# Weighted sum of two expert outputs: whole-tile VectorE instructions and results packed into the input tile

## The chip, the cores and the metric

The kernel runs on one core of one Trainium2 chip. The time is in device microseconds (us) of one execution; the median over several executions is what is compared. A profile of one execution, taken by the hardware, gives the span of the core, the busy time of each engine and every DMA's transfers. The span in a profile is about 2 us shorter than the time, since it starts with the first instruction.

Of the engines, VectorE (DVE) and ScalarE (ACT) compute here. SyncE (SP) only issues DMAs, and ScalarE issues DMAs too. Each of the two has a DMA queue of its own, and both queues are worked off by the same 16 DMA engines.

## The reference

Each of 16 x 1024 = 16384 tokens has the outputs of two experts, 512 values each, and two weights. The result is their weighted sum, in float32 throughout.

```python
batch, seq, hidden, n_experts, k = 16, 1024, 512, 8, 2
expert_outputs   # (batch, seq, k, hidden), float32
combine_weights  # (batch, seq, k), float32

def reference(expert_outputs, combine_weights):
    weights = combine_weights[..., np.newaxis]
    return np.sum(expert_outputs * weights, axis=2).astype(np.float32)
```

67.1 MB are read and 33.6 MB are written, with three arithmetic operations per result.

## The kernel before

128 partitions hold 128 tokens each, in 16 tiles of J = 8 tokens per partition. One tile is one load of 4 MB (32 KB per partition, contiguous in memory) and one store of 2 MB. Tiles are counted from 0; tile 15 is the last (`g == last`). Loads are issued by SyncE, stores by ScalarE, but for the four quarter stores of the last tile, which SyncE issues.

```python
    wpool = ctx.enter_context(tc.tile_pool(name="w", bufs=1))
    ipool = ctx.enter_context(tc.tile_pool(name="in", bufs=4))
    opool = ctx.enter_context(tc.tile_pool(name="out", bufs=4))

    wt = wpool.tile([P, per * k], dt)          # all weights, loaded once by two DMAs
    # ... cut: the two loads of wt, issued by ScalarE

    for g in range(per // J):
        et = ipool.tile([P, J, k * h], dt)     # 128 x 8 x 1024
        ot = opool.tile([P, J, h], dt)         # 128 x 8 x 512
        nc.sync.dma_start(out=et, in_=eo(g * J, J))
        c0 = 0
        for c in (2, 2, 2, 2) if g == last else (J,):
            for i in range(c0, c0 + c):
                t = g * J + i
                w0, w1 = wt[:, 2 * t : 2 * t + 1], wt[:, 2 * t + 1 : 2 * t + 2]
                if t == 0 or g == last:
                    nc.scalar.activation(out=ot[:, i, :], in_=et[:, i, 0:h], func=copy, scale=w0)
                else:
                    nc.vector.tensor_scalar_mul(out=ot[:, i, :], in0=et[:, i, 0:h], scalar1=w0)
                nc.vector.scalar_tensor_tensor(
                    out=ot[:, i, :], in0=et[:, i, h : 2 * h], scalar=w1, in1=ot[:, i, :],
                    op0=mult, op1=add,
                )
            (nc.sync if g == last else nc.scalar).dma_start(
                out=o(g * J + c0, c), in_=ot[:, c0 : c0 + c, :]
            )
            c0 += c
```

The kernel is written for a layer that orders the instructions of each engine by a scheduler of its own and sets the semaphores; a tile from a pool with `bufs=4` shares four buffers with the other tiles of that pool, and waits until the buffer it takes is no longer in use.

Of the kernel before, what the change touches and what calls it, by code (L numbers as in the profile page):

```python
# [1 line left out]

# [4 lines left out]


@with_exitstack
def kernel(  # L10
    ctx: ExitStack,
    tc: tile.TileContext,
    expert_outputs: bass.AP,
    combine_weights: bass.AP,
    out: bass.AP,
):

    nc = tc.nc  # L20
    b, s, k, h = expert_outputs.shape
    assert k == 2
    n = b * s
    P = nc.NUM_PARTITIONS
    per = n // P
    assert per * P == n
    J = 8
    main = per - J
    eo = expert_outputs.rearrange("b s k h -> (b s) (k h)")
    cw = combine_weights.rearrange("b s k -> (b s) k")  # L30
    o = out.rearrange("b s h -> (b s) h")

    def rows(x):

        a = x[0 : P * main, :].rearrange("(p t) f -> p t f", p=P)
        b = x[P * main : n, :].rearrange("(p t) f -> p t f", p=P)
        return lambda t, c: a[:, t : t + c, :] if t < main else b[:, t - main : t - main + c, :]

    eo, cw, o = rows(eo), rows(cw), rows(o)

    dt = mybir.dt.float32
    mult = mybir.AluOpType.mult
    add = mybir.AluOpType.add
    copy = mybir.ActivationFunctionType.Copy

    last = per // J - 1

    wpool = ctx.enter_context(tc.tile_pool(name="w", bufs=1))
    ipool = ctx.enter_context(tc.tile_pool(name="in", bufs=4))
    opool = ctx.enter_context(tc.tile_pool(name="out", bufs=4))  # L50

    wt = wpool.tile([P, per * k], dt)
    for t, c in ((0, main), (main, J)):
        nc.scalar.dma_start(
            out=wt[:, k * t : k * (t + c)].rearrange("p (t k) -> p t k", k=k), in_=cw(t, c)
        )

    for g in range(per // J):
        et = ipool.tile([P, J, k * h], dt)
        ot = opool.tile([P, J, h], dt)  # L60
        nc.sync.dma_start(out=et, in_=eo(g * J, J))  # L61
        c0 = 0
        for c in (2, 2, 2, 2) if g == last else (J,):
            for i in range(c0, c0 + c):
                t = g * J + i
                w0, w1 = wt[:, 2 * t : 2 * t + 1], wt[:, 2 * t + 1 : 2 * t + 2]


                if t == 0 or g == last:
                    nc.scalar.activation(out=ot[:, i, :], in_=et[:, i, 0:h], func=copy, scale=w0)  # L70
                else:
                    nc.vector.tensor_scalar_mul(out=ot[:, i, :], in0=et[:, i, 0:h], scalar1=w0)  # L72
                nc.vector.scalar_tensor_tensor(  # L73
                    out=ot[:, i, :],
                    in0=et[:, i, h : 2 * h],
                    scalar=w1,
                    in1=ot[:, i, :],
                    op0=mult,
                    op1=add,
                )  # L80

            (nc.sync if g == last else nc.scalar).dma_start(  # L82
                out=o(g * J + c0, c), in_=ot[:, c0 : c0 + c, :]
            )
            c0 += c


# [1 line left out]
_INS = ['expert_outputs', 'combine_weights']  # L89
_OUTS = [((16, 1024, 512), 'float32')]  # L90


# [23 lines left out]
```

## Time and profile before

| | |
|---|---|
| time, median of 3 runs | 241.44 us (241.16 to 241.47) |
| span of the profiled execution | 239.5 us |
| VectorE busy | 133.3 us, 56% of the span, 247 instructions |
| ScalarE busy | 7.0 us, 3%, 10 instructions |
| moved by DMA | 100.81 MB, mean 421 GB/s over the span |
| loads of a tile, issue to landing (min / median / max) | 12.6 / 49.5 / 50.5 us |
| stores, issue to landing (min / median / max) | 4.7 / 24.0 / 25.0 us |
| chain of work that ended last | DMA loads 56%, VectorE 26% of the span |
| first load landed, VectorE's first instruction | 13.37 us, 13.50 us |
| last store issued | 233.8 us |

Busy time counts an engine's instructions only, not what it waits for. A DMA's time to landing counts from its issue, so it holds the wait behind earlier DMAs of its queue as well as its own transfer. In the slices of the profile each digit is the busy share in tenths. Line numbers (L72, L73) are those of the kernel before: L72 is `tensor_scalar_mul`, L73 is `scalar_tensor_tensor`, L70 the activation, L61 the load, L82 the stores.

### The profile page before, as it was taken

The numbers are of one execution on the slowest core, as the hardware profiler recorded it, in microseconds if no ns is written. First come the engines' busy times: TensorE is split into PE (matmuls) and PEld (weight loads), VectorE is DVE, ScalarE is ACT, GpSimd is POOL, SyncE is SP. The second block draws the span as 40 slices with busy tenths as digits, with TensorE's granted clock in tenths as the row PEclk, the third lists the DMA queues.
The fourth block names the chain that finished last, engine by engine and source line by source line (L and its number), as shares of the span: only waits on it lengthen the run. The fifth ranks groups of instructions, "written<-read, shape, count | busy, mean of one in ns | idle before, by whom it ended". The sixth has DMA issues, their size and how long they took to land.

```text
span 239.5 us, 382 instructions
## 1 busy us (share of the span) xinstructions
DVE 133.3 (56%) x247; ACT 7.0 (3%) x10; POOL 0.2 (0%) x4
## 2 busy tenths in 40 slices
DVE  0077928529185490945819277291852918549080
ACT  0030000000000000000000000000000000000080
POOL 0000000000000000000000000000000000000000
DMA  7999899999999999999999999999999999999995
GB/s 268 451 441 439 350 438 476 401 432 424 411 441 435 479 394 438 435 441 400 435 438 441 435 460 413 438 402 432 437 435 479 397 438 427 449 397 435 438 409 213
DMA packets 5330, 100.81 MB, mean 421 GB/s; under 512 B 720, under 2 KB 848, under 8 KB 1360
## 3 DMA queue, kind: packets, MB, share of 16 engines
q1 hardware_dynamic: 2880, 69.21, 67.6%
q10 hardware_dynamic: 2448, 31.59, 30.9%
q14 instruction: 2, 0.02, 0.0%
HBM read 67.24 MB, written 33.55 MB: 421 GB/s over the span
## 4 chain that ended last, share of the span: by engine, by line
DMA 56%; DVE 26%; another core or an unknown queue 13%; issue 1%; SPq 0%; ACT 0%; DVEq 0%; ACTq 0%
DMA et<-in_expert_outputs_dram 56%; DVE ot L73 17%; DVE ot L72 10%; SPq L61 0%; ACT ot L70 0%; DVEq L111 0%; ACTq L82 0%; DVEq L72 0%; ACTq L70 0%
## 5 line engine op out<-in xcount | busy, mean ns | idle before, releaser
L72 DVE TENSOR_SCALAR ot<-et,wt 128x512 f32<-128x512 f32 x119 | 52.3, 481 | 93.7 <-DMA et<-in_expert_outputs_dram 80.2
L73 DVE SCALAR_TENSOR_TENSOR ot<-et,wt,ot 128x512 f32<-128x512 f32 x128 | 89.8, 745 | 6.7 <-ACT ot L70 6.7
L70 ACT ACTIVATE ot<-et,wt 128x512 f32<-128x512 f32 x9 | 5.7, 709 | 212.2 <-DMA et<-in_expert_outputs_dram 212.2
L70 ACT ACT_TABLE_LOAD x1 | 1.3, 1283 | 13.4 <-DMA et<-in_expert_outputs_dram 13.4
L100 POOL MEMSET const-bfloat16-1.0<- 128x1 bf16 x1 | 0.1, 102 | 0.0
L100 POOL MEMSET const-uint8-127<- 128x1 uint8 x1 | 0.1, 102 | 0.0
L100 POOL MEMSET const-float32-0.0<- 128x1 f32 x1 | 0.1, 99 | 0.2 <-issue 0.2
L100 POOL MEMSET const-float32-1.0<- 128x1 f32 x1 | 0.1, 99 | 0.0
## 6 DMA issues: line engine op xcount, KB each, us to landing
et<-in_expert_outputs_dram SPq DMA_DIRECT2D x16, 4096.0 KB, 49.5
out_dram<-ot ACTq DMA_DIRECT2D x15, 2048.0 KB, 24.1
out_dram<-ot SPq DMA_DIRECT2D x4, 512.0 KB, 4.9
wt<-in_combine_weights_dram ACTq DMA_DIRECT2D x1, 120.0 KB, 12.8
wt<-in_combine_weights_dram ACTq DMA_DIRECT2D x1, 8.0 KB, 22.1
```

The source lines that it names most:

```text
L70: nc.scalar.activation(out=ot[:, i, :], in_=et[:, i, 0:h], func=copy, scale=w0)
L72: nc.vector.tensor_scalar_mul(out=ot[:, i, :], in0=et[:, i, 0:h], scalar1=w0)
L73: nc.vector.scalar_tensor_tensor(out=ot[:, i, :], in0=et[:, i, h : 2 * h], scalar=w1, in1=ot[:, i, :], op0=mult, op1=add,)
L100: nc = _bacc.Bacc("TRN2", target_bir_lowering=False, num_devices=1)
```

## The change

Three things change together. First, each tile but the last is computed by two VectorE instructions in place of sixteen: one product of the whole tile with the weights, each weight repeated 512 times along its row by an access pattern of step 0, and one sum of the two halves of all eight tokens. Second, the result goes back into the input tile: the sum writes the eight results packed into the first half of `et`, so that each partition's 16 KB leave as one contiguous row. There is no output pool any more, and the freed memory makes six input buffers in place of four. Third, a tiny activation at the start brings ScalarE's table load forward. The last tile is still computed token by token by ScalarE and VectorE, with its results packed in place, and leaves in four quarters.

The aim is fewer and longer instructions on VectorE and loads that can run further ahead.

```diff
-    ipool = ctx.enter_context(tc.tile_pool(name="in", bufs=4))
-    opool = ctx.enter_context(tc.tile_pool(name="out", bufs=4))
+    ipool = ctx.enter_context(tc.tile_pool(name="in", bufs=6))
...
+    warm = wpool.tile([P, 1], dt)
+    nc.scalar.activation(out=warm, in_=nc.const_aps.tensor(1.0, (P, 1), dt), func=copy)
+
     for g in range(per // J):
         et = ipool.tile([P, J, k * h], dt)
-        ot = opool.tile([P, J, h], dt)
+        ot = et.rearrange("p j f -> p (j f)")[:, 0 : J * h].rearrange("p (j f) -> p j f", f=h)
         nc.sync.dma_start(out=et, in_=eo(g * J, J))
-        c0 = 0
-        for c in (2, 2, 2, 2) if g == last else (J,):
-            for i in range(c0, c0 + c):
...
-                if t == 0 or g == last:
-                    nc.scalar.activation(out=ot[:, i, :], in_=et[:, i, 0:h], func=copy, scale=w0)
-                else:
-                    nc.vector.tensor_scalar_mul(out=ot[:, i, :], in0=et[:, i, 0:h], scalar1=w0)
...
+        if g < last:
+            wb = wt[:, g * J * k : (g + 1) * J * k].unsqueeze(2).to_broadcast([P, J * k, h])
+            ek = et.rearrange("p j (k h) -> p (j k) h", k=k)
+            nc.vector.tensor_tensor(out=ek, in0=ek, in1=wb, op=mult)
+            nc.vector.tensor_tensor(out=ot, in0=et[:, :, 0:h], in1=et[:, :, h : 2 * h], op=add)
+            nc.scalar.dma_start(out=o(g * J, J), in_=ot)
+            continue
...
+        for c0 in range(0, J, 2):
+            for i in range(c0, c0 + 2):
+                t = g * J + i
+                nc.scalar.activation(
+                    out=et[:, i, 0:h], in_=et[:, i, 0:h], func=copy, scale=wt[:, 2 * t : 2 * t + 1]
+                )
                 nc.vector.scalar_tensor_tensor(
                     out=ot[:, i, :],
                     in0=et[:, i, h : 2 * h],
-                    scalar=w1,
-                    in1=ot[:, i, :],
+                    scalar=wt[:, 2 * t + 1 : 2 * t + 2],
+                    in1=et[:, i, 0:h],
                     op0=mult,
                     op1=add,
                 )
...
+            nc.sync.dma_start(out=o(g * J + c0, 2), in_=ot[:, c0 : c0 + 2, :])
```

## The prediction

> **What bounds the kernel now.** I read the page's table of slices first. Columns: one digit or number per 6 us slice.
>
> ```profile
> DVE  0077928529185490945819277291852918549080
> DMA  7999899999999999999999999999999999999995
> GB/s 268 451 441 439 350 438 476 401 432 424 411 441 435 479 394 438 435 441 400 435 438 441 435 460 413 438 402 432 437 435 479 397 438 427 449 397 435 438 409 213
> ```
>
> VectorE rests in every third slice; the DMA engines never do from the second slice to the last but one. Then the busy time by stages (stretch, its length, busy time and instruction count of each engine, clock, mean share of the 16 DMA engines, rate):
>
> ```profile
> 36.00:222.00 186.00, 111.24 (x208) 0.00 (x0) 0.00 (x0) 1.00 1.01 434
> 222.00:228.00 6.00, 0.00 (x0) 0.42 (x1) 0.00 (x0) 1.00 0.92 393
> 228.00:237.00 9.00, 5.39 (x8) 4.58 (x8) 0.00 (x0) 1.00 0.92 381
> 237.00:239.50 2.50, 0.00 (x0) 0.00 (x0) 0.00 (x0) 1.00 0.03 11
> ```
>
> In the long middle the rate is 434 GB/s at full DMA share, with VectorE busy 60%. Even while the last tile is computed (228 to 237) the engines are 0.92 full. Transfers run from about 1.6 to 237 us: 100.81 MB / 235.4 us = 428 GB/s on average. The bytes over that rate are the bound, and only time in which no transfer is queued can be added or removed. Next the queues and the DMA issues (median us to landing last):
>
> ```profile
> q1 hardware_dynamic: 2880, 69.21, 67.6%
> q10 hardware_dynamic: 2448, 31.59, 30.9%
> ...
> et<-in_expert_outputs_dram SPq DMA_DIRECT2D x16, 4096.0 KB, 49.5
> out_dram<-ot ACTq DMA_DIRECT2D x15, 2048.0 KB, 24.1
> ```
>
> A load is issued 49.5 us before it lands, over three tiles ahead, so the load queue is never empty. The packet counts give the arbitration: 16 loads x 128 rows + 4 last stores x 128 rows + 20 DMAs x 16 completions = 2880, and 15 x 128 + 256 + 17 x 16 = 2448. So a row is a packet: 32 KB in the load queue, 16 KB in the store queue. Last, the groups (count, then busy us and mean ns):
>
> ```profile
> L72 DVE TENSOR_SCALAR ot<-et,wt 128x512 f32<-128x512 f32 x119 | 52.3, 481 | 93.7 <-DMA et<-in_expert_outputs_dram 80.2
> L73 DVE SCALAR_TENSOR_TENSOR ot<-et,wt,ot 128x512 f32<-128x512 f32 x128 | 89.8, 745 | 6.7 <-ACT ot L70 6.7
> ```
>
> Neighbours overlap: in the timeline tile 2 runs from 36.86 to 45.41, so 8.55 us of VectorE per tile, against a load landing every (227.5 - 36.86) / 13 = 14.66 us.
>
> **What the Trainium skill says.** (1) "DMA: Bandwidth & Descriptors", section "Queues, rings and completion order": each DMA engine takes turns between its queues packet by packet. With rows of 32 and 16 KB that gives loads two thirds of the rate while stores are queued: 4.194 MB / (434 x 2/3) = 14.5 us per load, and the trace has 14.66. (2) The same page, "Where 436 GB/s comes from", puts the ceiling at 435 GB/s; the trace has 434, so no faster transfer is left to gain. (3) "VectorE: DVE Perf Modes", section "The TRN2 errata": an fp32 tensor_tensor takes (N + 151) / 0.96 ns. No tensor_tensor is in this trace, but the scalar_tensor_tensor, which also reads two fp32 streams, fits with N = 512: 691 ns by the formula, 745 in the trace. (4) "SBUF — State Buffer", section "SBUF: two separate sides": engines and DMA do not slow each other there. The trace agrees loosely: the rate of a slice does not follow VectorE's digit.
>
> **The change part by part.** *VectorE.* Per tile, 16 instructions go and 2 come: a product over 8192 elements and a sum over 4096. 512 elements at 0.96 per ns are 533 ns of the 745, so the fixed part is 212 ns; the product is then an estimated 8533 + 212 = 8.75 us and the sum 4267 + 212 = 4.48 us, together 13.2 us in place of 8.55. For 15 tiles that is +70 us of VectorE work, but 13.2 is still under 14.66, so it hides beside transfers. Fewer instructions save nothing that counts.
>
> *Buffers.* 4 x 32 KB + 4 x 16 KB per partition become 6 x 32 KB. A load now waits for the landing of the store six tiles earlier, not for the arithmetic four tiles earlier. Around a buffer: 13.2 (arithmetic) + about 24 (store) leave 6 x 14.66 - 37 = 51 us for the load. Before it was 49.5. The load queue stays filled: 0 us.
>
> *Table load and warm-up.* The 1.28 us table load sat at 13.4 us beside the wait for the first load; moving it forward gains at most a little for tile 0, whose activation goes anyway: 0 us.
>
> *Order.* The scheduler rearranges the end, and this is the part that counts. In the built program VectorE no longer goes tile by tile there: product 11, product 12, sum 11, sum 12, product 13, product 14, sum 13, sum 14. ScalarE, which issues the stores, has two activations of tile 15 ahead of the stores of tiles 13 and 14. In the kernel before all 15 stores came first. So store 11 waits for load 12, and stores 13 and 14 wait for load 15.
>
> I work the times out with these units: 14.66 us for a load beside stores (and for a store beside loads), two thirds of it, 9.77, for a load alone, a third, 4.89, for a store alone; about 1.5 us from last byte to landing and 1 us from issue to first byte (estimates: the last store is issued at 233.8 and takes 4.7 to land, of which its 0.52 MB need 1.2 and the quarter ahead of it may take another 1). For the kernel before they give load 2 landing at 37.1; the trace has 36.86.
>
> - Load 0 lands at 13.4 as before; tile 0 ends at 26.7 and store 0's first byte is at 27.6 (before 22.7). Loads run alone 5 us longer, so load 2 lands at 34.6, load k at 34.6 + 14.66 (k - 2): load 11 at 166.5, load 12 at 181.2.
> - Stores follow without a gap, so store 10's bytes end at 27.6 + 11 x 14.66 = 188.9.
> - Product 11 ends at 175.3, product 12 waits for load 12 and ends at 190.0, sum 11 at 194.4, sum 12 at 198.9. Store 11 starts at 195.4. From 188.9 loads are alone, at full rate: nothing lost, only shifted. Load 13 lands at 194.0, load 14's bytes end at 205.7, load 15's at 220.4; it lands at 221.9.
> - Stores 11 and 12 share with loads until 220.4; the rest of store 12, 30% or 1.4 us, ends at 221.8.
> - Sum 13 is done at 220.9, but its store waits behind two activations, which start when load 15 lands: 221.9 + 0.62 + 0.72 = 223.2, first byte at 224.2. Between 221.8 and 224.2 no transfer is queued: **2.4 us lost**.
> - After that stores 13, 14 and 15 (6.3 MB, 14.6 us) run without gaps, as sum 14 ends at 225.4 and the quarters of tile 15 follow within some 6 us.
>
> Sum: 0 + 0 + 0 + 2.4, so 241.4 + 2.4 = 243.8; I lean a little to the short side, as the gap can close: 243.7.
>
> **Rivals.** (a) The gap closes: if store 12 is a little further behind, it is still moving when store 13 is issued, and nothing is lost: 241.4. For it: only 1.4 us of store 12 covers the hole, and 2.5 us more would fill it. Against it: the shares are calibrated to a trace that matches 2:1. (b) VectorE becomes the bound. If the product, with a weight repeated 512 times as second operand, or the sum, written over its own input, takes more than an element per cycle, 13.2 can pass 14.66. Its chain alone, from 13.5 us over 15 tiles, the last tile's 5.4 and the 5.8 us that the trace has from VectorE's end to the span's end, plus 2 us from span to time, gives 13.5 + 15 x + 13.2: 244 for 14.5 us per tile, 255 for 15.2, some 350 if the product takes two cycles per element (21.8). For it: nothing of that form is in the trace. Against it: the two-input instruction here runs at 533 ns plus a constant. (c) Loads starve with stores inside the buffer's round trip. Against it: 51 us of room; it would need a store to take over 60 us. (d) Faster: stores later means more loads at the start at full rate, but the rate in total is 434 either way, so a shift of bytes buys no time; at the most the 0.92 of the last stages is filled up, 15 x 0.08 = 1.2 us: 240.2.
>
> **Range and chances.** (a) at 241.4 bounds the range below; above, a store 12 that ends as load 15's bytes do would make the gap 3.8, and a VectorE that is late by another 1 to 1.5 us there brings 246: 241.0 to 246.4. The limit of 2% is 246.3, which by the chain's formula needs VectorE 1.4 us per tile slower than estimated: 0.12. Faster than 236.6 would need over 435 GB/s: 0.02. The rest, 0.86, is within 2%.
>
> **What would show it.** Right: groups of about 8.75 and 4.48 us on VectorE, load rate and 14.66 us spacing kept, a DMA share of 1 to about 222 us, and there a hole of 2 to 3 us with ScalarE's two activations just before the next store. Wrong: VectorE busy in all slices (rival b), a hole in the middle (c), or no hole at the end and a time at 241.4 (a). My weakest steps are the tensor_tensor's length, which no trace here shows, and the 1.4 us of store 12.

## The result, and the profile after

| | before | changed |
|---|---|---|
| time, median | 241.26 us (241.16 to 241.47, 6 runs) | 240.49 us (240.32 to 240.89, 6 runs) |
| ratio to before | | 0.997, 95% interval 0.9957 to 0.9983 |
| span of the profiled execution | 239.5 us | 238.4 us |
| VectorE busy | 133.3 us in 247 instructions | 201.3 us in 38 instructions |

The changed kernel is 0.3% faster. I had predicted 243.7 us, in a range from 241.0 to 246.4: the time lies 0.5 us below the range. The profile is that of the fastest of the six executions (240.32 us).

The slices of the changed kernel's page, one per 6 us, answer to those of the kernel before:

```profile
DVE  0069999999999998989979799797927999999940
ACT  2000000000000000000000000000000000000620
DMA  7999999999999999999999999999999999999997
```

VectorE has almost no rests any more. The DMA share is as before but for the last slice. By stages (stretch, length, busy time and instructions of each engine, clock, DMA share, rate):

```profile
36.00:222.00 186.00, 171.98 (x27) 1.14 (x2) 0.00 (x0) 1.00 1.00 433
222.00:228.00 6.00, 5.79 (x8) 3.98 (x7) 0.00 (x0) 1.00 1.01 429
228.00:237.00 9.00, 1.38 (x3) 0.00 (x0) 0.00 (x0) 1.00 0.97 399
```

The middle has the same 433 to 434 GB/s. What differs is the end: 1.01 and 0.97 where the kernel before had 0.92 and 0.92. The groups on VectorE:

```profile
L69 DVE TENSOR_TENSOR et<-et,wt 128x8192 f32<-128x8192 f32 x15 | 130.3, 8689 | 27.5 <-DMA wt<-in_combine_weights_dram 13.7
L70 DVE TENSOR_TENSOR et<-et 128x4096 f32<-128x4096 f32 x15 | 66.2, 4423 | 0.4
```

**Where the time went.** The last two microseconds show it. First the kernel before, then the changed one, same columns as above:

```profile
236.00:237.00 1.00, 0.00 (x0) 0.00 (x0) 0.00 (x0) 1.00 0.44 176
237.00:238.00 1.00, 0.00 (x0) 0.00 (x0) 0.00 (x0) 1.00 0.07 29
```

```profile
236.00:237.00 1.00, 0.00 (x0) 0.00 (x0) 0.00 (x0) 1.00 0.81 324
237.00:238.00 1.00, 0.00 (x0) 0.00 (x0) 0.00 (x0) 1.00 0.00 0
```

A share of 0.07 for a whole microsecond is one DMA engine out of 16 (1/16 = 0.06) still at work after the others have stopped. Each DMA leaves 16 completion records in the trace, which I take as one from each engine. In the kernel before, the last store's first fifteen are in by 237.09 us and the sixteenth at 238.45: 1.36 us later. In the changed kernel they are at 237.35 and 237.37. So the straggler gives 1.34 us, the other fifteen take back 0.26, and 1.08 us is what the last landing gains; the spans differ by 1.1.

Followed back, the sixteenth record of each DMA trails the fifteenth by 0.03 us or less up to the store that lands at 40.5 us, by 0.6 to 0.8 from the load at 52.2 to the store at 172.0, and by 1.4 to 1.6 from the load at 183.9 on. The two steps fall on two packets of a third DMA queue, at 47.2 and 173.5 us. On the page of the kernel before it has one line, which I had passed over (queue, kind, packets, MB, share):

```profile
q14 instruction: 2, 0.02, 0.0%
```

The page of the changed kernel has no such line; there are two queues only:

```profile
q1 hardware_dynamic: 2880, 69.21, 68.0%
q10 hardware_dynamic: 2448, 31.59, 31.0%
```

These packets are 8 KB of a program each, fetched while the kernel runs. That is some 128 instructions: in gpsimd_900 (below) GpSimd starts 125 to 142 of its memsets between one fetch and the next. A VectorE program of 247 instructions needed two of them; one of 38 needs none. The first theory therefore is: **instruction fetches put one DMA engine behind, and since no engine is ever idle here, it stays behind to the end.** Rivals: the packing in place, the six buffers, the early table load, or stores that start later.

### The profile page after: what moved, and what is told of

The parts are those of the page before. It is cut to its first block, busy times and chain, and to the rows that moved or that the text cites. A ratio compares the mean times of both kernels' runs of the same rounds, so it can differ in the third digit from the quotient of the medians.

```text
span 238.4 us, 177 instructions
## 1 busy us (share of the span) xinstructions
DVE 201.3 (84%) x38; ACT 6.6 (3%) x10; POOL 0.2 (0%) x4
## 4 chain that ended last, share of the span: by engine, by line
DMA 65%; DVE 29%; ACT 1%; ACTq 0%; DVEq 0%; issue 0%; SPq 0%
DMA et<-in_expert_outputs_dram 38%; DMA out_dram<-et 21%; DVE et L69 18%; DVE et L70 10%; DMA wt<-in_combine_weights_dram 5%; ACT et L78 1%; DVE et L81 1%; DVEq L115 0%; ACTq L115 0%; ACTq L71 0%; SPq L64 0%; DVEq L81 0%
## 5 line engine op out<-in xcount | busy, mean ns | idle before, releaser
L69 DVE TENSOR_TENSOR et<-et,wt 128x8192 f32<-128x8192 f32 x15 | 130.3, 8689 | 27.5 <-DMA wt<-in_combine_weights_dram 13.7
L70 DVE TENSOR_TENSOR et<-et 128x4096 f32<-128x4096 f32 x15 | 66.2, 4423 | 0.4
L78 ACT ACTIVATE et<-et,wt 128x512 f32<-128x512 f32 x8 | 5.1, 710 | 219.6 <-DMA et<-in_expert_outputs_dram 217.7
L81 DVE SCALAR_TENSOR_TENSOR et<-et,wt 128x512 f32<-128x512 f32 x8 | 5.6, 748 | 0.2
## 6 DMA issues: line engine op xcount, KB each, us to landing
et<-in_expert_outputs_dram SPq DMA_DIRECT2D x16, 4096.0 KB, 47.2
```

What stands on the lines that cost most here:

```text
L69: nc.vector.tensor_tensor(out=ek, in0=ek, in1=wb, op=mult)
L70: nc.vector.tensor_tensor(out=ot, in0=et[:, :, 0:h], in1=et[:, :, h : 2 * h], op=add)
L78: nc.scalar.activation(out=et[:, i, 0:h], in_=et[:, i, 0:h], func=copy, scale=wt[:, 2 * t : 2 * t + 1])
L81: nc.vector.scalar_tensor_tensor(out=ot[:, i, :], in0=et[:, i, h : 2 * h], scalar=wt[:, 2 * t + 1 : 2 * t + 2], in1=et[:, i, 0:h], op0=mul ...
```

## Experiments

Ratios are to the kernel before, run beside each on the same chip. A fetch is an 8 KB packet of the instruction queue.

| run | time, us | ratio, 95% interval | fetches in the span |
|---|---|---|---|
| few_instr | 240.18 | 0.9959 (0.9945 to 0.9972) | 0 |
| many_in_place | 241.33 | 1.0002 (0.9994 to 1.001) | 2 |
| half_of_the_tiles | 240.97 | 0.9985 (0.9978 to 0.9991) | 1 |
| before_plus_600 | 245.17 | 1.0162 (1.0148 to 1.0175) | 7 |
| gpsimd_900 | 244.17 | 1.012 (1.0106 to 1.0134) | 7 |
| scalar_pass | 242.52 | 1.0048 (1.0034 to 1.0062) | 0 |
| late_stores_on_sync | 240.37 | 0.9958 (0.9945 to 0.9972) | 0 |
| four_buffers | 243.49 | 1.0074 (1.0051 to 1.0097) | 0 |
| three_buffers | 251.6 (one execution) | | 0 |
| one_last_store, one_last_store_2 | 240.19, 240.32 | 0.9951 (0.9938 to 0.9963), 0.9957 (0.9945 to 0.997) | 0 |
| few_one_last_store, and again | 239.66, 240.10 | 0.9935 (0.9923 to 0.9948), 0.9945 (0.9933 to 0.9958) | 0 |
| few_one_late_on_sync | 239.66 | 0.993 (0.9917 to 0.9942) | 0 |
| changed_again, changed_third | 240.71, 240.82 | 0.9969 (0.9958 to 0.9979), 0.9978 (0.997 to 0.9985) | 0 |

### Which part of the change gives the time

*few_instr* is the kernel before with the new arithmetic alone, in its old buffers:

```diff
         ot = opool.tile([P, J, h], dt)          # four buffers each, as before
+        if g < last:
+            wb = wt[:, g * J * k : (g + 1) * J * k].unsqueeze(2).to_broadcast([P, J * k, h])
+            ek = et.rearrange("p j (k h) -> p (j k) h", k=k)
+            nc.vector.tensor_tensor(out=ek, in0=ek, in1=wb, op=mult)
+            nc.vector.tensor_tensor(out=ot, in0=et[:, :, 0:h], in1=et[:, :, h : 2 * h], op=add)
+            nc.scalar.dma_start(out=o(g * J, J), in_=ot)
+            continue
```

> The kernel before with its four input and four output buffers, but each of the first 15 tiles computed by one product over 8192 elements (in place in the input tile) and one sum over 4096 (into the output tile). Theory 1 (instruction fetch): with some 40 VectorE instructions in place of 247 there is no 8 KB instruction fetch inside the span (2 in the kernel before), no DMA engine runs 1.4 us behind the other fifteen at the end, and the time is 240.2 to 240.7. Rival (buffers): the gain came from results packed in place and six buffers, which this kernel lacks: 241.2 to 241.5, with the lag still there.

*many_in_place* is the opposite: everything of the change but the whole-tile arithmetic.

```diff
-            nc.vector.tensor_tensor(out=ek, in0=ek, in1=wb, op=mult)
-            nc.vector.tensor_tensor(out=ot, in0=et[:, :, 0:h], in1=et[:, :, h : 2 * h], op=add)
+            for i in range(J):
+                t = g * J + i
+                nc.vector.tensor_scalar_mul(out=et[:, i, 0:h], in0=et[:, i, 0:h], scalar1=wt[:, 2 * t : 2 * t + 1])
+                nc.vector.scalar_tensor_tensor(out=ot[:, i, :], in0=et[:, i, h : 2 * h],
+                    scalar=wt[:, 2 * t + 1 : 2 * t + 2], in1=et[:, i, 0:h], op0=mult, op1=add)
```

> The changed kernel with its six buffers, results packed in place and early table load, but the first 15 tiles computed token by token with 16 VectorE instructions each, as before. Theory 1 (instruction fetch): 2 instruction fetches of 8 KB inside the span again, one DMA engine 1.3 to 1.9 us behind at the end, 241.0 to 241.7. Rival (buffers, packing or the early table load): as the changed kernel, 240.3 to 240.7. A third view, that stores which start later (26.9 in place of 21.7 us) gave the gain, expects 241.3 here too, as VectorE takes 8.6 us per tile again, but without a lagging DMA engine.

240.18 and 241.33 us: the whole-tile arithmetic carries the whole gain, and packing, six buffers and the early table load carry none of it. In many_in_place one engine is again 1.5 us behind the fifteenth when load 15 lands and 1.0 behind at the end; in few_instr 0.01 at the end. Near the end of many_in_place the lone engine shows:

```profile
237.00:238.00 1.00, 0.00 (x0) 0.00 (x0) 0.00 (x0) 1.00 0.06 25
```

The whole-tile arithmetic also makes the stores start later and brings the new order at the end, and these two runs don't part the fetches from that. What speaks for the fetches is that the fifteen other engines end no earlier in the changed kernel, but 0.26 us later, and that further fetches, added to the kernel before or to the changed one, cost 3.4 to 3.9 us (below). A record that trails is no proof by itself: in many_in_place store 0 trails by 1.1 us before the first fetch. In the kernel before, the lag grows at the two fetches and lasts.

*half_of_the_tiles* takes the token-by-token form for tiles 0 to 7 only (`if g < 8:` around the loop above, the two instructions otherwise), which makes 150 VectorE instructions.

> The changed kernel with tiles 0 to 7 token by token (16 VectorE instructions) and tiles 8 to 14 by two: 150 VectorE instructions. Theory 1: one instruction fetch inside the span, near 47 us, one DMA engine about 0.7 us behind from there to the end, 240.7 to 241.1, between the changed kernel and the one before. Rival (only a program above some length is slowed, or the fetches are harmless): as the changed kernel within 0.1 us and no lag.

240.97, between the two, with one fetch, at 46.6 us. In store 13 the sixteenth record trails by 0.75 us. I had expected the lag to last to the end, and it doesn't: in the profiled execution, the fastest of 21 (240.44), it is 0.25 us in store 14 and 0.03 in the last store. Store 14 waits for load 15 here, which leaves a short hole just before it:

```profile
226.00:227.00 1.00, 0.18 (x1) 0.94 (x2) 0.00 (x0) 1.00 0.66 279
```

So the time of this run holds a hole as well as a fetch, and its interval touches that of the changed kernel beside it (changed_again). It fits the theory and does not test it.

### More fetches than the kernel has

*before_plus_600* adds instructions that nothing needs:

```diff
+    scr = wpool.tile([P, 128], dt)
...
             c0 += c
+        if g < last:
+            for j in range(40):
+                nc.vector.tensor_copy(out=scr[:, j : j + 1], in_=ot[:, 7, j : j + 1])
```

> The kernel before with 40 further VectorE copies of one column to a scratch tile after each of the first 15 tiles: 847 VectorE instructions, and under 13 us of VectorE work per tile, still less than the 14.66 between loads. Theory 1 (instruction fetch): 4 to 5 more fetches of 8 KB (128 instructions each), 6 to 7 in all; if all pass through one DMA engine at some 0.8 us each, it is about 5 us behind at the end and the time is 244 to 246. Rival (VectorE's work is hidden, fetches harm nothing): 241.2 to 241.6.

The copies take 37.7 us of VectorE in all, 2.5 per tile, so a tile takes some 11 us and still fits between loads. The queue's line and the stages at the end:

```profile
q14 instruction: 7, 0.06, 0.1%
...
225.00:231.00 6.00, 2.19 (x37) 0.00 (x0) 0.00 (x0) 1.00 1.01 430
231.00:234.00 3.00, 1.64 (x3) 2.39 (x4) 0.00 (x0) 1.00 0.11 44
234.00:237.00 3.00, 3.00 (x5) 2.61 (x5) 0.00 (x0) 1.00 0.79 320
```

Seven fetches, five more than in the kernel before; from the second on, the trailing engine is 1.1, 1.9, 2.6, 3.4, 4.2 and 4.9 us behind as they add up. The fifteenth record stays within 0.5 us of the fourteenth, so it is one engine. The stretch from 231 to 234 shows how this turns into time: load 15 lands on fifteen engines at 226.5 us and on the last at 231.5, and the last tile can't be computed before that. Fifteen engines run dry in the meantime: share 0.11. As they wait too, only 1.8 us of the lag are left at the last store.

*gpsimd_900* puts 900 one-column memsets on GpSimd, which otherwise has four instructions:

```diff
+    scr = wpool.tile([P, 128], dt)
+    for j in range(900):
+        nc.gpsimd.memset(scr[:, j % 128 : j % 128 + 1], 0.0)
```

> The changed kernel with 900 one-column memsets to a scratch tile on GpSimd, which nothing waits for. Theory 1 for any engine's program: about 7 fetches of 8 KB, one DMA engine 4 to 6 us behind at the end, 244 to 246. Rival: only VectorE's own instruction stream matters, or GpSimd's fetches are spread over several DMA engines: 240.3 to 241.5.

```profile
q14 instruction: 7, 0.06, 0.1%
...
222.00:224.00 2.00, 2.00 (x2) 0.00 (x0) 0.00 (x0) 1.00 0.08 33
224.00:226.00 2.00, 2.00 (x2) 1.33 (x2) 0.00 (x0) 1.00 0.37 156
```

It isn't VectorE's work, nor its program alone: seven fetches of another engine's program, all before 40 us and for instructions that nothing waits for, cost 3.4 to 3.7 us (244.17 against 240.49 to 240.82). Load 15 lands at 224.49 in place of 220.86, with the other engines dry before that. Here the delay isn't all on one engine: in load 15 the fifteenth record comes 1.3 us after the fourteenth, and the sixteenth another 5.0. At the last store 0.04 us are left, not the 4 to 6 that I had expected.

### The hole that I had predicted

The timeline of the changed kernel near the end (start, length, engine, line and operation; idle time before in brackets):

```profile
206.33 8.69 DVE L69 TENSOR_TENSOR et<-et,wt 128x8192 f32<-128x8192 f32 x1
214.94 8.75 DVE L70 TENSOR_TENSOR et<-et 128x4096 f32<-128x4096 f32 x2
220.86 0.72 ACT L78 ACTIVATE et<-et,wt 128x512 f32<-128x512 f32 x1 [217.72 <-DMA et<-in_expert_outputs_dram]
220.92 0.34 ACTq L71 DMA_DIRECT2D out_dram<-et  x1
221.49 0.71 ACT L78 ACTIVATE et<-et,wt 128x512 f32<-128x512 f32 x1
223.61 5.77 DVE L81 SCALAR_TENSOR_TENSOR et<-et,wt 128x512 f32<-128x512 f32 x8
223.72 0.34 ACTq L71 DMA_DIRECT2D out_dram<-et  x1
```

Sum 13 is done at 219.4, and its store does wait for load 15, as the order in the program says. But it is issued 0.06 us after the first of the two activations ahead of it has started, and before the second has: it doesn't wait for their 1.34 us. The Trainium skill has half of this, in "Perfetto Trace Analysis", section "Sequencer Loop": an engine's sequencer pushes an engine instruction into a queue, and it is the engine instruction that waits for its semaphores. The trace agrees in that no activation's end held the store up. By the loop alone, though, the store could have gone out at 219.4, when its sum was done; measured is 220.92, once load 15 had let the first activation start. What is left of the hole in this profile is nothing: from 221 to 222 us the DMA share is 0.96.

*scalar_pass* makes the two stores depend on an activation that stands behind tile 15's: ScalarE copies one row of 512 results of tiles 13 and 14 over itself.

```diff
+            if g >= last - 2:
+                nc.scalar.activation(out=ot[:, J - 1, :], in_=ot[:, J - 1, :], func=copy)
             nc.scalar.dma_start(out=o(g * J, J), in_=ot)
```

> The changed kernel, but ScalarE copies the last token row of tiles 13 and 14 over itself before their stores, so that these two stores truly wait for an activation that stands behind two of tile 15's. Theory: a store that only stands behind activations is issued without waiting for their end, so the hole that I predicted did not appear; here it does: store 13 is issued some 2 us after load 15 lands (about 223), store 12 has ended by about 221.5, so 1 to 2.5 us without a transfer, and the time is 241.5 to 243. Rival (the queued bytes of store 12 would have covered any such wait): no hole, 240.3 to 240.8.

```profile
220.00:222.00 2.00, 2.00 (x1) 0.85 (x2) 0.00 (x0) 1.00 0.73 311
222.00:224.00 2.00, 2.00 (x2) 1.62 (x4) 0.00 (x0) 1.00 0.27 115
...
222.39 0.61 ACT L72 ACTIVATE et<-et 128x512 f32<-128x512 f32 x1
222.91 0.70 ACT L80 ACTIVATE et<-et,wt 128x512 f32<-128x512 f32 x1
223.04 0.34 ACTq L73 DMA_DIRECT2D out_dram<-et  x1
```

With a wait of that length the hole appears, where I had put it and of about that size: 2 x (0.27 + 0.73) = 2.0 us lost, and the time is 1.7 to 2.0 us above the changed kernel's medians (240.49 to 240.82).

Executions of the changed kernel lie further apart (240.49 to 241.08 in changed_third) than those of the kernel before, and in the profile of changed_third a small hole stands in the same place:

```profile
221.00:222.00 1.00, 1.00 (x1) 0.59 (x1) 0.00 (x0) 1.00 0.69 295
```

Load 15 lands at 221.39 us there, its sixteenth record 0.6 after the fifteenth, against 220.84 and 0.1 in the profile without a hole. No fetch is behind this lag; why it comes and goes, the runs don't show.

*late_stores_on_sync* lets SyncE issue the stores of tiles 13 and 14, so that nothing of load 15's landing stands ahead of them:

```diff
-            nc.scalar.dma_start(out=o(g * J, J), in_=ot)
+            (nc.sync if g >= last - 2 else nc.scalar).dma_start(out=o(g * J, J), in_=ot)
```

> The changed kernel, but the stores of tiles 13 and 14 are issued by SyncE, in whose queue they stand behind load 15 itself and not behind its landing. Theory: what is left of the predicted hole (DMA share 0.62 from 221 to 222 us in one profile of the changed kernel, about 0.4 us) depends on the execution and is the reason why executions lie 0.7 us apart; here store 13 is issued when its sum ends, near 219.5, no microsecond near 221 has a share under 0.8, and the median falls by 0.2 to 0.6, all executions within 0.3. Rival (the scatter comes from the DMA engines themselves): the same median and scatter as the changed kernel.

> The changed kernel itself beside the next three: 240.2 to 240.9, with single executions some 0.7 us apart, as seen before.

```profile
219.75 4.68 SPq L71 DMA_DIRECT2D out_dram<-et  x2
...
221.00:222.00 1.00, 1.00 (x1) 0.76 (x2) 0.00 (x0) 1.00 1.04 442
```

Store 13 leaves at 219.75 in place of 221.48, the hole is gone, the median falls from 240.82 to 240.37 and the executions lie within 0.23 us. The intervals overlap, from 0.997 to 0.9972, so the size (0.45) is less sure than the hole.

### Buffers

> The changed kernel with four input buffers in place of six. By the sum that I used for the buffers, 4 x 14.66 = 58.6 us around a buffer less 13.1 for the arithmetic and about 24.7 for the store leave 21 us for a load that needs 14.7 beside stores: never empty, time 240.3 to 241. Rival (loads starve from six down): 245 or more, holes in the DMA share.

> The changed kernel with three input buffers. The same sum: 3 x 14.66 = 44 less 13.1 less 24.7 leave 6 us for a load that needs at least 9.7 alone; the load queue runs empty at each tile, and tiles come every 15 to 18 us: 250 to 285. Rival: stores shorten as soon as they do not queue behind one another, and three buffers still hold the rate: 241 to 245.

Only `bufs=6` becomes 4 or 3. Four buffers: 243.49, against my 240.3 to 241. By stages, in the slowest of four executions (243.97), with the issue of load 15:

```profile
36.00:205.00 169.00, 153.97 (x24) 0.00 (x0) 0.00 (x0) 1.00 1.01 430
...
222.00:224.00 2.00, 2.00 (x1) 0.00 (x0) 0.00 (x0) 1.00 0.19 82
224.00:226.00 2.00, 1.90 (x3) 1.78 (x3) 0.00 (x0) 1.00 0.62 262
...
209.59 0.33 SPq L64 DMA_DIRECT2D et<-in_expert_outputs_dram  x1
```

In the steady part the sum holds: 430 GB/s. It says nothing of the end, where sum 11 stands behind product 12: load 15 waits for the late store 11, is issued at 209.59 and lands at 224.2, store 13 waits for it, and 2.4 us (2 x (0.81 + 0.38)) have no transfer. With three buffers it is 251.6 us, as expected. The load queue does run empty, at about every second tile: load 8 is issued at 116.41 us, 0.26 after load 7 has landed. Stores fill most of these pauses, as the DMA share from 36 to 222 us is still 1.00, but the rate there is 411 GB/s in place of 433.

### A faster version

*one_last_store* sends the last tile's 2 MB in one store when all of it is ready.

```diff
-            nc.sync.dma_start(out=o(g * J + c0, 2), in_=ot[:, c0 : c0 + 2, :])
+            if c0 == J - 2:
+                nc.sync.dma_start(out=o(g * J, J), in_=ot)
```

> The changed kernel with one store of 2 MB for the last tile in place of four of 0.5 MB. In the changed kernel stores 13 and 14 are still moving when tile 15 is complete at 229.4, so the quarters gain nothing by leaving early; their rows of 4 KB move at 159 to 166 ns each (412 GB/s over 16 engines), rows of 16 KB at 611 ns (429). Theory: 2.1 MB cost 4.9 in place of 5.1 to 5.3 us and the time falls by 0.2 to 0.4 to 240.1 to 240.3. Rival: the last store is no longer overlapped and its start is late: 241 or more.

> The changed kernel with one store for the last tile, beside the changed kernel itself. Theory (rows of 4 KB move at 412 GB/s, the quarters leave no earlier than the queue ahead of them): 0.2 to 0.4 us less than the changed kernel. Rival: the same within 0.1 us, as both wait for the same queue.

> The changed kernel itself, on the same chip as the next three: 240.2 to 240.9.

240.32 beside the changed kernel's 240.71 on one chip: the sign is as expected, the intervals overlap. That the longer rows are the reason isn't shown. Two more kernels put things together: *few_one_last_store* is few_instr with one last store, *few_one_late_on_sync* adds SyncE's stores of tiles 13 and 14.

> Two instructions per tile with four input and four output buffers, and one store for the last tile: if the number of instructions and the row length of the last stores are all that counts, 239.9 to 240.3, as the changed kernel with one last store. If packing in place and six buffers are worth something of their own, 0.3 us or more above that.

> Two instructions per tile, four input and four output buffers and one last store, a second time: 239.6 to 240.3. If separate output buffers are worth something of their own, again 239.7 or less; if the last result was chance, between 239.7 and 240.3.

> The same, with the stores of tiles 13 and 14 issued by SyncE: no fetch, no hole, long rows at the end. Theory: 239.4 to 239.8 in every execution, the fastest of all. Rival: the same as the one before it within its scatter.

The first gave 239.66, less than the 239.9 to 240.3 that I had expected, and, on another chip, 240.10 with executions from 239.64 to 240.31; its second profile has the hole again (share 0.62 from 221 to 222). With the hole closed: 239.66, all five executions between 239.54 and 239.76, 0.993 of the kernel before. Its interval (0.9917 to 0.9942) lies below that of the changed kernel beside it (0.997 to 0.9985): it beats both. The end of its profile:

```profile
236.00:237.00 1.00, 0.00 (x0) 0.00 (x0) 0.00 (x0) 1.00 0.09 33
237.00:238.00 1.00, 0.00 (x0) 0.00 (x0) 0.00 (x0) 1.00 0.00 0
```

## Why the prediction was wrong

Two steps failed, the price of 0 us for fewer instructions (measured: 1.1 us saved) and the store that waits for the end of two activations (2.4 us, measured: 0 to 0.4). With both put right the sum is 241.4 - 1.1 + 0 to 0.4 = 240.3 to 240.7, and the medians are 240.49 to 240.82.

**The bound: right.** The rate in the middle is 434 before and 433 after, and no experiment went past it.

**VectorE's instructions: right.** 8.75 and 4.48 us estimated, 8.689 and 4.423 measured; the skill's formula that I cited gives 8.691 and 4.424. A weight with step 0 as second operand and writing over the own input cost nothing extra, so rival (b) fell.

**"Fewer instructions save nothing that counts": this step failed.** I priced instructions by VectorE's time alone. Some 128 of them are also an 8 KB transfer through the resource that bounds the kernel. The two fetches put one DMA engine 1.36 us behind at the end; without them the span fell by 1.1 us. The runs with 0, 2 and 7 fetches show it from both sides. The profile had both hints: the line of the instruction queue, and the 0.92 at the end, which I took for a loose average; the microsecond after it, at 0.07, is one engine.

**The end's timeline: right to about 1 us.** Product 12 was to wait for load 12 at 181.2 (180.26), load 15 to land at 221.9 (220.84), and store 13 to wait for it.

**The hole of 2.4 us: right mechanism, wrong size.** The failed term is "its store waits behind two activations ... 221.9 + 0.62 + 0.72": measured 0.06 in place of 1.34 us. My 1.5 us from a load's last byte to its landing was 0.96 (last packet of load 15 ends at 219.88). These two make 1.8 of the 2.4; what is left varies between nothing and about 0.4 us. With these two right I would have said 242.0, and the missing 1.1 us of the fetches would still have been an error in the sign.

**Buffers: right for six.** A load has 47.2 us from issue to landing where I had left 51. The formula failed at four because it describes the steady part only.

**Rivals.** (a), no hole at 241.4, was nearest in what happens, for the reason it gave only in part: it was the early issue more than store 12. (d) named 240.2 as a floor by filling the 0.92; the number is close by luck, as the cause wasn't a shift of bytes. The sign that I gave for (b), VectorE busy in all slices, did appear, and (b) was false all the same. At the start the loads are ahead of VectorE, so it works without a rest for 13.1 us per tile until, near 93 us, it has caught up. From then on the products start 14.5 us apart, each after a wait for its load:

```profile
107.55 8.69 DVE L69 TENSOR_TENSOR et<-et,wt 128x8192 f32<-128x8192 f32 x1 [1.40 <-DMA et<-in_expert_outputs_dram]
122.09 8.69 DVE L69 TENSOR_TENSOR et<-et,wt 128x8192 f32<-128x8192 f32 x1 [1.39 <-DMA et<-in_expert_outputs_dram]
```

**Open.** A fetch's packet takes 0.31 us, but leaves its engine some 0.8 behind; the traces don't say what the rest is. The first fetch of before_plus_600, at 26.7 us, left only 0.15. Why the other fifteen engines end 0.26 us later in the changed kernel, I haven't traced.

## What to carry to other kernels

When the DMA engines never rest, as here, what one of them does besides can stay on the clock to the end: look at the last engine, not at the mean, by the share of the last microseconds (1/16 is one engine) and by the sixteenth completion of a DMA. Then a long program is itself a cost: one 8 KB fetch for some 128 instructions, here on VectorE and on GpSimd, even for instructions that nobody waits for. And where a scheduler puts a store behind instructions that wait for the last load, see in the timeline what the store really waits for, their start or their end, before giving it a price.

## What was not expected of the hardware

- Seven 8 KB fetches, 0.06% of the bytes, cost 3.4 to 3.7 us (gpsimd_900), and five more than the two of the kernel before cost 3.9 (before_plus_600). The Trainium skill, "Runtime: NRT & Kernel Launch", section "Instruction fetch mechanics", calls the cost of a fetch "mostly hidden" and gives blocks of 16 KiB; here they are packets of 8 KB, and in a kernel bound by DMA they are not hidden. The measurement decides.
- A DMA issue on ScalarE's queue went out 0.06 us after the start of an activation ahead of it, while a second one ahead had not started. Its data had been ready since 219.4 us; it left only when load 15 had landed.
- Rows of 4 KB moved at 159 ns each and engine in the kernel before (median), 412 GB/s over 16; rows of 16 KB at 611 ns, 429 GB/s; rows of 32 KB at 1213 ns, 432 GB/s.
